# A Hyena and neighbourhood-attention step: the even half of each forward transform moved ahead by half a round, the second quarter's gates moved into the attention stage, row-wise products and outer taps on VectorE

## The chip, the cores and the metric

The kernel runs on 1 core of one Trainium2 chip. The metric is the device time of one execution in microseconds (us), lower is better. The engines are named as the profile names them: PE (TensorE, matrix products), PEld (its weight loads), DVE (VectorE), ACT (ScalarE), POOL (GpSimd) and SP (SyncE, which issues most of the transfers).

## The reference, cut to what matters

One layer of a backbone on 128 context tokens and 512 latent tokens with 1024 channels. Both token groups go through two branches that share one input projection; the kernel handles them together as rows of 640 columns (128 + 512).

```python
z = h @ w_in                              # hy, g_h, qkv, g_a, m
hy = short_conv(hy, conv_w, conv_b)       # 3 taps along the sequence
v_h, x1, x0 = split(hy, 3)
u = v_h * x1
uf = rfft(u, n=2 * L); ff = rfft(filt_full, n=2 * L)
y = irfft(uf * ff)[:, :L]                 # long convolution
y_h = (y + u * d_bias) * x0
y_a = attention(q, k, v)                  # windows and cached context keys
p_h = (y_h * silu(g_h)) @ w_bh
p_a = (y_a * silu(g_a)) @ w_ba
out = (sigmoid(m_h) * p_h + sigmoid(m_a) * p_a) @ w_out
x = layer_norm(ALPHA * x + gate * out)
```

## The kernel before, in words

All products are done in three passes of fp32r halves: a weight tile is split into a high part `wh` and a low part `wl`, the input into `hH` and `hL`, and the passes are wh·hH, wh·hL, wl·hH. A projection tile (`proj`, L184) is 128 channels by 640 tokens: 8 k-steps of 6 matmuls of 128x320, 48 in all, into two PSUM banks named `mm<i>_0` and `mm<i>_1` (pool of four banks, so two tiles at a time). Its weights come in on SP, ACT makes `wl` (a negated copy, L158), a DMA issued by POOL adds the raw tile to it (L159), and ACT makes `wh` (L160). There are two `wh` buffers, so the copy for a tile waits until the tile before the last no longer reads its own.

**The Hyena stage** goes in four rounds, a quarter q = 2 channel tiles each. `weave` (L75) lays a main chain of projections and a side chain of transforms beside each other by counting steps. The main chain of round q is `quarter_head(q + 1)` (tiles n and 8 + n, whose product is u) and `quarter_tail(q)` (L595: tiles 16 + n, which give x0, and, except where q is in `LATE_GATES`, tiles 24 + n, the gates). A `conv_tile` (L545) copies its banks to a padded row `zs` on ACT, applies the centre tap on ACT (L557) and the outer two taps either as two DVE operations (L563) or, with `taps=True`, as an ACT copy into `tap` (L560) and a POOL add (L561). `gate_tile` (L570) takes tanh on ACT (L573) and a product on DVE (L568). `gapped_product` (L538) multiplies gate row and x0 row in three POOL operations.

The side chain of round q is `gated_conv(q - 1)` (L700: transposes `yp`, `y` of the result of the last inverse transform, and products on DVE), `long_conv(q)` (L613: transposes `ut` of the rows u, split into `uh` on ACT and `ul` on DVE; class products `c0`, `s0`, then `c1`, `s1`, then `p_X`; sums and the spectrum products on DVE), and `long_conv_back(q)` braided with `filter_spectrum(q + 1)` (`fl`, `sd`, `sh`/`sl`, `fa` ... `fp`). Side products go into a second pool of four banks (`aux`, L103). In this stage the order on each engine is not written out: a scheduler with its own costs decides it from the program and its dependencies, and each engine then runs its queue strictly in that order.

**The attention stage** has 8 blocks j. In each, `attend(j)` is woven with two or three `pair_tile`s (L1183), which compute two projection tiles by a Strassen-like scheme: 7 products of 12 matmuls of 128x320 instead of 96, so 84, at the price of weight sums (L1158) and result sums (L1207, L1213) on DVE. PE's order is written out here, that of ACT and DVE is the scheduler's. `mains` (L1355) is the table of pairs by block. For the quarter in `LATE_GATES` (quarter 0 before) the x0 row is kept, the product y·x0 goes to `yu_d` in memory, and `gates_h(m)` (L1239) loads it back, multiplies by the gate and stores it to `yh_d`. `GATED_AT` (L1286) names the pairs that also compute one row of the final gate (L1307).

Of the kernel before, what the change touches and what calls it, by code (L numbers as in the profile page):

```python
# [16 lines left out]
LP = 128  # L17
# [16 lines left out]

LATE_GATES = (0,)

# [12 lines left out]
def tile_hyena_natten_step(ctx: ExitStack, tc: tile.TileContext, a, o):  # L49
# [370 lines left out]
    def filter_spectrum(q):  # L420
# [36 lines left out]
        def halves(name, sd):  # L457
            sh = hw.tile([P, 2, 256], F32R, tag="shl", bufs=4, name=f"sh{q}_{name}")
            sl = hw.tile([P, 2, 256], F32R, tag="shl", bufs=4, name=f"sl{q}_{name}")
            split(sh[:], sl[:], sd[:])  # L460
            return [(sh[:, i], sl[:, i]) for i in range(2)]
# [114 lines left out]
    def quarter_head(q):  # L576
        us = []
        out[f"u{q}"] = us
        for i in range(2):
            n = 2 * q + i  # L580
            u = hw.tile([P, ROW], F32, tag="u", bufs=4, name=f"u{n}")
            x1 = hwa.tile([P, ROW], F32, tag="cv", bufs=2, name=f"x1_{n}")
            tiles = ((n, u), (8 + n, x1))
            if q == 3 and i == 0:
                tiles = tiles[::-1]
            yield from conv_tile(*tiles[0])
            yield
            yield from conv_tile(*tiles[1])
            nc.vector.tensor_tensor(u[:, :NG], u[:, :NG], x1[:, :NG], op=ALU.mult)
            us.append(u)  # L590
            yield
# [21 lines left out]
    def long_conv(q):  # L613
        us, F, ident = out[f"u{q}"], out[f"F{q}"], out["ident"]
        if q == 0:
            dft_inverse()

# [9 lines left out]

        X = hw.tile([P, 10, 256], F32, tag="X", name=f"X{q}")
        E = out[f"E{q}"] = hw.tile([P, 12, 256], F32, tag="E", name=f"E{q}")
        e, plus, minus = E[:, :4], E[:, 4:8], E[:, 8:]  # L630
        for g in range(2):
            srcs = [src(2 * g), src(2 * g + 1)]
            yield
# [4 lines left out]
            if g == 0:  # L638
                nc.scalar.activation(e[:, 0:2], two(pc[:]), AF.Copy)
                nc.scalar.activation(e[:, 2:4], two(psn[:]), AF.Copy)  # L640
            else:
                nc.vector.tensor_tensor(plus[:, 0:2], e[:, 0:2], two(pc[:]), op=ALU.add)
                nc.vector.tensor_tensor(minus[:, 0:4:3], e[:, 0:2], two(pc[:]), op=ALU.subtract)
                nc.vector.tensor_tensor(plus[:, 2:4], e[:, 2:4], two(psn[:]), op=ALU.add)
                nc.vector.tensor_tensor(minus[:, 1:3], e[:, 2:4], two(psn[:]), op=ALU.subtract)
            yield
        s4 = src(4)
        pp = aux(f"p_X{q}")
# [19 lines left out]
    def long_conv_back(q):  # L668
# [15 lines left out]
        for g, rs_ in enumerate(((0, 2), (1, 3), (4,))):  # L684
            pb = aux(f"yb{q}_{g}")
            dst = ye[:, 2 * g : 2 * g + 2] if g < 2 else yp
            for i, r in enumerate(rs_):
                s = pq[:, r : r + 6 : 5] if r < 4 else R[:, 4:10:5]
                ph = hw.tile([P, 2, 256], F32R, tag="shl", bufs=4, name=f"ph{q}_{r}")
                pl = hw.tile([P, 2, 256], F32R, tag="shl", bufs=4, name=f"pl{q}_{r}")  # L690
# [9 lines left out]
    def gated_conv(q):  # L700
# [7 lines left out]
        for i in range(2):  # L708
# [6 lines left out]
            if q in LATE_GATES:  # L715
                x0, s0 = out["yh"][n], SC if q == 3 else GAP
                yh = hw.tile([P, ROW], F32, tag="u", bufs=4, name=f"yu{n}")[:, :NT] if q == 3 else row(yhp, "yh", f"yu{n}")
# [549 lines left out]
    def qk_(j):  # L1267
        return T_Q + j, T_K + j
# [7 lines left out]
    def mix_(m):  # L1276
# [78 lines left out]
    def mains(j):  # L1355
# [11 lines left out]
    with tc.manual_schedule(engines={mybir.EngineType.PE}):  # L1367
# [376 lines left out]
```

## Time and profile before

| | |
|---|---|
| median of 3 runs | 861.82 us (859.06, 861.82, 863.29) |
| the profiled execution, its own time | 859.01 us |
| its span in the trace | 857.0 us |
| granted clock of TensorE | 0.998 of full speed |
| PE busy / PEld busy | 847.1 / 820.6 us |
| DVE / ACT / POOL busy | 684.8 / 476.8 / 176.5 us |

The span is the time from the first to the last instruction in the trace; 2.0 us of the execution's own time lie around it. An engine's busy time counts its instructions; since consecutive instructions of ACT and DVE overlap by about a tenth of a microsecond, what one costs in a queue is read from the start of one to the start of the next in the timeline. The same holds for matmuls, whose ends are modelled.

### The profile page before, as it was taken

Reading aid. Unit: us, or ns where it says so; the run is one execution under the profiler, and the core shown is the slowest. Engines: PE = TensorE matmul, PEld = TensorE weight load, DVE = VectorE, ACT = ScalarE, POOL = GpSimd, SP = SyncE. Lnnn points to the kernel's source line nnn. Section 1 sums busy time; section 2 is a strip of 40 time slices with the busy share of each in tenths; the row PEclk is TensorE's granted clock in tenths of the full one; section 3 lists DMA queues with packets and bytes.
Section 4 is the critical chain, followed back from the end, with each engine's and each line's share of the span. In section 5 each row is a group of like instructions: output and inputs, shape, how many; then the busy total and the mean of one; then the engine's idle time right before and its main releaser. Section 6 shows DMA issues by size and latency. Waiting matters only on the chain.

```text
span 857.0 us, 16856 instructions
## 1 busy us (share of the span) xinstructions
PE 847.1 (99%) x6375; PEld 820.6 (96%) x6375; DVE 684.8 (80%) x1388; ACT 476.8 (56%) x1016; POOL 176.5 (21%) x172
## 2 busy tenths in 40 slices
PE   9999999999999999999999999999999999999996
PEld 7999999999999999999999999999999999999885
DVE  6677695597778558989988897888888668799676
ACT  4675666646557445565565576656656554345310
POOL 0010230341345201042123235124222200000000
PEclk9999999999999999999999999999999999999999
DMA  9986565666647668764353535444253375545631
GB/s 351 366 246 149 112 147 114 158 129 142 144 98 158 124 170 216 214 202 132 101 179 89 192 103 182 122 166 158 91 180 112 124 248 210 183 121 148 227 123 50
DMA packets 57443, 138.90 MB, mean 162 GB/s; under 512 B 8559, under 2 KB 24435, under 8 KB 57364
## 3 DMA queue, kind: packets, MB, share of 16 engines
q1 hardware_dynamic: 45700, 112.34, 39.6%
q0 software_dynamic: 5472, 19.14, 13.6%
q10 hardware_dynamic: 6192, 6.36, 2.1%
q8 instruction: 50, 0.82, 0.4%
q14 instruction: 29, 0.24, 0.1%
HBM read 121.04 MB, written 16.78 MB: 161 GB/s over the span
## 4 chain that ended last, share of the span: by engine, by line
PE 97%; DVE 1%; DMA 1%; SPq 0%; issue 0%; DVEq 0%
PE sp L1198 34%; PE mm L179 31%; PE out L1567 6%; PE v L934 5%; PE pt L1036 3%; PE s L1043 3%; PE s L996 2%; PE mm L193 2%; PE ve L946 1%; DMA ada<-wada 1%; PE adaT L264 1%; PE yb L169 1%; PE yb L167 1%; PE yb L168 1%; PE fl L445 1%; PE ut L622 1%
## 5 line engine op out<-in xcount | busy, mean ns | idle before, releaser
L1198 PE MATMUL sp<-t,wb 128*128 128x320 f32 x960 | 149.7, 310 | 0.0
L1198 PEld LDWEIGHTS sp<-t,wb 128*128 128x128 f32 x960 | 142.0, 188 | 1.3 <-ACT pp L1064 0.3
L1198 PE MATMUL sp<-hH,wb 128*128 128x320 f32 x480 | 116.4, 313 | 0.0
L179 PE MATMUL mm<-hH,wl 128*128 128x320 f32 x416 | 97.7, 309 | 0.0
L179 PE MATMUL mm<-hH,wh 128*128 128x320 f32 x416 | 96.9, 310 | 0.0
L179 PE MATMUL mm<-hL,wh 128*128 128x320 f32 x416 | 96.4, 309 | 0.0
L110 ACT ACTIVATE wb<-s 128x512 fp32r<-128x512 f32 x96 | 58.7, 627 | 49.3 <-DVE s L1158 25.3
L1198 PEld LDWEIGHTS sp<-hH,wb 128*128 128x128 f32 x480 | 82.4, 188 | 2.1 <-issue 2.0
L159 POOL DMA_DIRECT2D wl<-wall x35 | 30.6, 875 | 240.1 <-ACT wl L158 208.1
L1198 PE MATMUL sp<-hL,wb 128*128 128x320 f32 x240 | 74.0, 309 | 0.0
L179 PEld LDWEIGHTS mm<-hH,wl 128*128 128x128 f32 x416 | 70.3, 188 | 0.8
L179 PEld LDWEIGHTS mm<-hL,wh 128*128 128x128 f32 x416 | 69.7, 188 | 0.4
L179 PEld LDWEIGHTS mm<-hH,wh 128*128 128x128 f32 x416 | 69.6, 188 | 0.3
L111 DVE TENSOR_TENSOR wb<-s,wb 128x512 fp32r<-128x512 f32 x96 | 64.7, 686 | 6.3 <-ACT wb L110 6.2
L110 ACT ACTIVATE wb<-raw 128x512 fp32r<-128x512 f32 x69 | 43.3, 627 | 47.2 <-PE sp L1198 26.8
L160 ACT ACTIVATE wh<-raw 128x1024 fp32r<-128x1024 f32 x35 | 37.1, 1061 | 56.4 <-PE mm L179 48.2
L1018 POOL TENSOR_SCALAR p<-p,sm 128x384 f32<-128x384 f32 x32 | 44.8, 1410 | 106.1 <-DVE sm L1017 106.1
L111 DVE TENSOR_TENSOR wb<-raw,wb 128x512 fp32r<-128x512 f32 x69 | 48.3, 700 | 4.9 <-ACT wb L110 4.6
L179 PE MATMUL mm<-yhs,wh 128*128 128x320 f32 x256 | 47.9, 309 | 0.0
L1198 PEld LDWEIGHTS sp<-hL,wb 128*128 128x128 f32 x240 | 45.1, 188 | 0.0
L1213 DVE TENSOR_TENSOR c<-sp,u 128x320 f32<-128x320 f32 x72 | 34.7, 481 | 12.6 <-PE sp L1198 12.6
L1018 POOL TENSOR_SCALAR edge<-edge,sm 128x320 f32<-128x320 f32 x32 | 42.1, 1325 | 0.4 <-PE sp L1198 0.2
(397 smaller groups left out, 2133.7 us busy)
## 6 DMA issues: line engine op xcount, KB each, us to landing
raw<-wall SPq DMA_DIRECT2D x93, 512.0 KB, 3.7
wl<-wall POOLq DMA_DIRECT2D x35, 512.0 KB, 6.0
ada<-wada SPq DMA_DIRECT2D x16, 512.0 KB, 9.1
tm<-bias SPq DMA_DIRECT2D x16, 512.0 KB, 4.5
xw<-xw SPq DMA_DIRECT2D x8, 512.0 KB, 9.5
gate<-wgate SPq DMA_DIRECT2D x8, 512.0 KB, 3.8
wo<-wall SPq DMA_DIRECT2D x8, 512.0 KB, 4.5
dec<-decay SPq DMA_DIRECT2D x20, 128.0 KB, 2.2
```

Source lines behind the costliest of these rows:

```text
L110: hi = nc.scalar.activation(dst_h, src, AF.Copy)
L111: return hi, (eng or nc.vector).tensor_tensor(dst_l, src, f(dst_h), op=ALU.subtract)
L159: nc.gpsimd.dma_start(wl, a["wall"][i], accum_op=ALU.add)
L160: nc.scalar.activation(wh, raw[:], AF.Copy)
L179: nc.tensor.matmul(ps[hf][:, :HALF], wt[k], x[:, hf * HALF : (hf + 1) * HALF], start=(i == 0 and k == 0), stop=(i == lead[2] and k == NK - ...
L934: nc.tensor.matmul(ps[t // 2][:, t % 2 * 256 : t % 2 * 256 + 256], x[:, k, P * t : P * t + P], wk, start=first and t % 2 == 0, stop=last, ...
L1018: nc.gpsimd.tensor_scalar_mul(pv, pv, sm[:, 2:3])
L1036: nc.tensor.transpose(pt[:, i * P : i * P + P], x, ident)
L1043: nc.tensor.matmul(dst, lhs, rhs, start=start, stop=stop, skip_group_check=True)
L1198: nc.tensor.matmul(dst, wk, x(xi, k), start=j < 4 and k == 0 and i == 0, stop=k == 3 and i == 2, skip_group_check=True,)
L1213: after = nc.vector.tensor_tensor(c, dst, c if j == 3 else u, op=ALU.add)
L1567: ins = nc.tensor.matmul(dst, m[k][:, c0 : c0 + P], w[:, c : c + n], start=(first and k == 0), stop=(last and k == 5), skip_group_check=True,)
```

## The change

- `LATE_GATES` becomes (0, 1). The gates of quarter 1 (tiles 26 and 27, 2 x 48 matmuls) leave round 1 and come back as one `pair_tile`, `gates_h(1)` (84 matmuls), in block j = 3 of attention, which so has three pairs. The x0 rows of quarters 0 and 1 are now rows of `yhp` in the compact form (two pieces per tap, 128 and 512 columns).
- `taps=False` everywhere: the outer taps of all x0 tiles are DVE operations; the ACT copies `tap` and the POOL adds go.
- `gapped_product` (now for quarters 2 and 3 only, 4 tiles instead of 6) moves from POOL to DVE.
- `long_conv` is cut in two: `long_conv_front(q + 1)` (transposes of classes 0 to 3, products `c0`, `s0`, ACT copies into a tile `e` of its own) stands at the end of the side chain of round q; the rest stays at the head of round q + 1, behind `gated_conv(q)`. The halves `sh`, `sl`, `ph`, `pl` get six buffers instead of four.
- `EARLY_VALUES` is empty: `early_values` yields nothing.

In sum PE has 6009 matmuls instead of 6021, DVE 56 operations more, ACT 4 fewer, POOL 36 fewer (no tensor operation is left on it in the Hyena stage).

```diff
-LATE_GATES = (0,)
+LATE_GATES = (0, 1)
+EARLY_VALUES = {}
...
     def gapped_product(y, x):
-        nc.gpsimd.tensor_tensor(y[:, :LP], y[:, :LP], x[:, :LP], op=ALU.mult)
+        nc.vector.tensor_tensor(y[:, :LP], y[:, :LP], x[:, :LP], op=ALU.mult)
...
-            nc.gpsimd.tensor_tensor(ys, ys, src, op=ALU.mult)
+            nc.vector.tensor_tensor(ys, ys, src, op=ALU.mult)
...
             if q in LATE_GATES:
-                x0 = row(yhp, "yh", f"x0_{n}") if q == 3 else hwa.tile([P, ROW], F32, tag="x0", bufs=2, name=f"x0_{n}")
-                yield from conv_tile(16 + n, x0, q == 3, True)
+                x0 = row(yhp, "yh", f"x0_{n}")
+                yield from conv_tile(16 + n, x0, True, False)
...
-                yield from conv_tile(16 + n, x0, taps=True)
+                yield from conv_tile(16 + n, x0, taps=False)
...
+    def long_conv_front(q):
...
+        while len(us) < 2:
             yield
+        srcs = [src(0), src(1)]
+        yield
+        pc, psn = pairs(0, srcs)
+        e = hw.tile([P, 4, 256], F32, tag="e", name=f"e{q}")
+        nc.scalar.activation(e[:, 0:2], two(pc[:]), AF.Copy)
+        nc.scalar.activation(e[:, 2:4], two(psn[:]), AF.Copy)
+        yield
+        fronts[q] = e, [src(2), src(3)], src, pairs
+        yield
+
+    def long_conv(q):
...
+        if q not in fronts:
+            yield from long_conv_front(q)
+        e, srcs, src, pairs = fronts.pop(q)
...
+    for q in range(3):
+        weave(chain(quarter_head(q + 1), quarter_tail(q), early_values(q)), chain(gated_conv(q - 1) if q else (), long_conv(q), braid(long_conv_back(q), filter_spectrum(q + 1)), long_conv_front(q + 1)),
...
-            qk_(1), ga_(0), qk_(2), mix_(0), gh_(0), qk_(3), mix_(1), ga_(2), qk_(4), mix_(2), qk_(5), mix_(3), ga_(4), ...
+            qk_(1), ga_(0), qk_(2), mix_(0), gh_(0), qk_(3), mix_(1), ga_(2), qk_(4), mix_(2), gh_(1), qk_(5), mix_(3), ga_(4), ...
...
-            3: ((queries_keys(4), mix(2)), 2 * N_PAIR),
+            3: ((queries_keys(4), mix(2), gates_h(1)), 3 * N_PAIR),
```

The orders are read where round 1 ends and round 2 begins. Tiles 20 and 21 are the x0 tiles of quarter 2, 28 and 29 its gates (rows `yh4`, `yh5`), 22 and 30 the same of the next channel tile; `ut2_4` is the transpose of the context columns of u of quarter 2, `uh2_4` its high half.

**Place A: ACT at the gates of tile 29.** Before:

```order
L110 ACTIVATE uh2_4_2602<-ut2_4_2599 128x256
L560 ACTIVATE tap2_21_0_3141<-zs0_107,pack2_602 128x641
L160 ACTIVATE wh30_3355<-raw30_3353 128x1024
L573 ACTIVATE yh5_3162<-mm29_0_3170 128x320
L573 ACTIVATE yh5_3162<-mm29_1_3171 128x320
L158 ACTIVATE wl23_3469<-raw23_3466 128x1024
L650 ACTIVATE X2_2471<-p_X2_2606 128x2x256
```

With the change:

```order
L161 ACTIVATE wh30_3263<-raw30_3261 128x1024
L159 ACTIVATE wl23_3350<-raw23_3347 128x1024
L574 ACT_TABLE_LOAD
L574 ACTIVATE yh4_2829<-mm28_0_2837 128x320
L574 ACTIVATE yh4_2829<-mm28_1_2838 128x320
L574 ACTIVATE yh5_3056<-mm29_0_3064 128x320
L574 ACTIVATE yh5_3056<-mm29_1_3065 128x320
L111 ACTIVATE uh2_4_2421<-ut2_4_2418 128x256
L551 ACTIVATE zs1_111<-mm22_0_3160 128x128
```

The four tanh of tiles 28 and 29 stand together, behind both weight copies and behind the load of the tanh table (which before stands at tile 26, in round 1), and `uh2_4` stands behind them; before, it stood ahead of `wh30` and of the tanh of tile 29.

**Place B: PE at the same time**, from `ut2_4` to `p_X2`, which reads `uh2_4`. Before:

```order
L169 MATMUL s1_X2_2570<-uh2_3_2553,dftL_104 128x256
L622 MATMUL ut2_4_2599<-pack2_602,u4_1568 128x128
L622 MATMUL ut2_4_2599<-pack2_602,u5_1807 128x128
L179 MATMUL mm29_0_3170<-hL_89,wh29_3165 128x320
L179 MATMUL mm29_1_3171<-hL_89,wh29_3165 128x320
```

With the change:

```order
L170 MATMUL s1_X2_2389<-uh2_3_2288,dftL_104 128x256
L623 MATMUL ut2_4_2418<-pack2_602,u4_1612 128x128
L623 MATMUL ut2_4_2418<-pack2_602,u5_1840 128x128
L168 MATMUL p_X2_2425<-uh2_4_2421,dftH_103 128x256
L445 MATMUL fl3_0_2572<-w3h_3_2565,hid_94 128x512
L446 MATMUL fl3_0_2572<-w3l_3_2566,hid_94 128x512
L180 MATMUL mm22_0_3160<-hH_88,wh22_3155 128x320
```

Before, 26 projection matmuls of tile 29 stand between the transposes `ut2_4` and `p_X2`; now `p_X2` follows the transposes at once, and ahead of them stand, after the last matmul of tile 29, the ten transposes `yp1`, `y2`, `y3` and the twelve products `c1`, `s1` of quarter 2 in one piece.

**Place C: ACT at the last piece of the filter spectrum of quarter 2**, `sh2_4`, which PE's `fp2` reads. Before:

```order
L110 ACTIVATE w3h_3_2746<-w3s3_2748 128x512
L110 ACTIVATE sh2_4_2321<-sd4_2_2318 128x512
L560 ACTIVATE tap2_20_0_2908<-zs2_115,pack2_602 128x641
L160 ACTIVATE wh29_3165<-raw29_3163 128x1024
L573 ACTIVATE yh4_2911<-mm28_0_2919 128x320
```

With the change:

```order
L111 ACTIVATE w3h_3_2565<-w3s3_2567 128x512
L161 ACTIVATE wh22_3155<-raw22_3153 128x1024
L111 ACTIVATE sh2_4_2158<-sd4_2_2155 128x512
L551 ACTIVATE zs0_107<-mm21_0_2950 128x128
L553 ACTIVATE zs0_107<-mm21_0_2950 128x8x8
```

Before, `sh2_4` followed `w3h_3` at once; now the weight copy `wh22` stands between them. `wh22` takes the buffer of tile 21's weights, so it waits for that tile's matmuls.

## Rows read from the trace of the kernel before

**Rows 1.** The page: span, busy time of the engines, the chain that ended last by engine.

```profile
span 857.0 us, 16856 instructions
PE 847.1 (99%) x6375; PEld 820.6 (96%) x6375; DVE 684.8 (80%) x1388; ACT 476.8 (56%) x1016; POOL 176.5 (21%) x172
...
PE 97%; DVE 1%; DMA 1%; SPq 0%; issue 0%; DVEq 0%
```

**Rows 2.** Busy time by stretch of 40 us through the Hyena stage; last line: sums.

```profile
200.00:240.00 40.00, 40.00 (x289) 39.82 (x288) 24.21 (x46) 25.01 (x47) 8.58 (x9) 1.00 0.57 132
...
sum 320.00, PE 320.00 PEld 318.10 DVE 240.20 ACT 191.98 POOL 77.05; mean PE 40.00 PEld 39.76 DVE 30.02 ACT 24.00 POOL 9.63
```

**Rows 3.** The chain of waits: start, us, what; a projection piece and a pair piece.

```profile
686.84 28.16 PE mm L179 x192
745.01 45.78 PE sp L1198 x312
```

**Rows 4.** Timeline of PE at the end of round 1: start, us, what.

```profile
221.33 0.40 PE L445 MATMUL fl<-w3l,hid 128*128 128x512 f32 x1
221.56 0.31 PE L179 MATMUL mm<-hH,wh 128*128 128x320 f32 x1
...
222.00 0.28 PE L168 MATMUL fd<-sl,gsH 128*128 128x256 f32 x1
222.12 0.28 PE L169 MATMUL fd<-sh,gsL 128*128 128x256 f32 x1
...
228.12 0.38 PE L707 MATMUL yp<-pack,E 128*128 128x128 f32 x2
...
228.69 0.54 PE L179 MATMUL mm<-hH,wh 128*128 128x320 f32 x2
```

**Rows 5.** Timeline of DVE at the same place.

```profile
221.76 0.69 DVE L450 TENSOR_TENSOR sd<-fl,dec 128x512 f32<-128x512 f32 x1 [1.51 <-PE fl L445]
222.37 0.75 DVE L436 TENSOR_TENSOR w3s<-w 128x256 f32<-128x256 f32 x2
```

**Rows 6.** Timeline of ACT at the same place.

```profile
223.57 0.67 ACT L110 ACTIVATE w3h<-w3s 128x512 fp32r<-128x512 f32 x1
224.09 0.67 ACT L110 ACTIVATE sh<-sd 128x512 fp32r<-128x512 f32 x1
```

**Rows 7.** Timeline of ACT where tile 26's gates load the tanh table.

```profile
155.56 1.07 ACT L160 ACTIVATE wh<-raw 128x1024 fp32r<-128x1024 f32 x1 [1.37 <-PE mm L179]
156.53 1.04 ACT L158 ACTIVATE wl<-raw 128x1024 fp32r<-128x1024 f32 x1
157.59 1.28 ACT L573 ACT_TABLE_LOAD   x1
158.88 0.77 ACT L573 ACTIVATE yh<-mm 128x320 f32<-128x320 f32 x2
159.53 0.60 ACT L519 ACTIVATE F<-fp 128x512 f32<-128x512 f32 x1
```

**Rows 8.** Groups of ACT, 40 to 360 us: busy, mean ns, idle before.

```profile
L160 ACT ACTIVATE wh<-raw 128x1024 fp32r<-128x1024 f32 x35 | 37.1, 1061 | 56.4 <-PE mm L179 48.2 <-PE ve L946 7.4 <-PE mm L193 0.7
L110 ACT ACTIVATE uh<-ut 128x256 fp32r<-128x256 f32 x20 | 7.3, 395 | 9.6 <-PE ut L622 9.4
```

**Rows 9.** Groups of DVE in the same stretch.

```profile
L111 DVE TENSOR_TENSOR sl<-sd,sh 128x512 fp32r<-128x512 f32 x24 | 24.0, 1000 | 13.5 <-ACT sh L110 13.4
L563 DVE SCALAR_TENSOR_TENSOR x<-zs,pack,x 128x641 f32<-128x641 f32 x16 | 14.1, 882 | 1.9 <-ACT x L557 1.7
```

**Rows 10.** Groups of POOL in the same stretch.

```profile
L561 POOL TENSOR_TENSOR x<-x,tap 128x641 f32<-128x641 f32 x16 | 30.2, 1887 | 11.5 <-ACT tap L560 11.5
L543 POOL TENSOR_TENSOR yh<-yh,x 128x448 f32<-128x448 f32 x6 | 8.7, 1449 | 0.2 <-DVE yh L568 0.2
```

**Rows 11.** Busy time in attention: block 1 (three pairs) and block 3 (two).

```profile
401.00:447.00 46.00, 45.95 (x362) 44.52 (x358) 40.39 (x101) 27.61 (x71) 11.62 (x10) 1.00 0.43 139
...
493.00:528.00 35.00, 35.00 (x287) 33.82 (x286) 31.39 (x89) 24.25 (x64) 12.10 (x10) 1.00 0.51 155
```

**Rows 12.** Groups of DVE, 400 to 800 us.

```profile
L111 DVE TENSOR_TENSOR wb<-s,wb 128x512 fp32r<-128x512 f32 x86 | 57.9, 686 | 5.2 <-ACT wb L110 5.1
...
L1213 DVE TENSOR_TENSOR c<-sp,u 128x320 f32<-128x320 f32 x65 | 31.3, 482 | 12.6 <-PE sp L1198 12.6
```

**Rows 13.** The chain of waits inside block 1: a run of pieces on DVE.

```profile
413.77 0.49 DVE c L1213
...
418.60 0.69 DVE wb L111
```

More of the change, by code (lines that the diff above doesn't have):

```diff
@@ L457, in halves @@
         def halves(name, sd):
-            sh = hw.tile([P, 2, 256], F32R, tag="shl", bufs=4, name=f"sh{q}_{name}")
-            sl = hw.tile([P, 2, 256], F32R, tag="shl", bufs=4, name=f"sl{q}_{name}")
+            sh = hw.tile([P, 2, 256], F32R, tag="shl", bufs=6, name=f"sh{q}_{name}")
+            sl = hw.tile([P, 2, 256], F32R, tag="shl", bufs=6, name=f"sl{q}_{name}")
             split(sh[:], sl[:], sd[:])
@@ L576, in quarter_head @@
     def quarter_head(q):
-        us = []
-        out[f"u{q}"] = us
+        us = out.setdefault(f"u{q}", [])
         for i in range(2):
@@ L611, in quarter_tail @@
             yield
[L613 to L616, printed above, removed]
+    fronts = {}
+    def long_conv_front(q):
+        ident = out["ident"]
+        us = out.setdefault(f"u{q}", [])
         def src(cls):
@@ L626, in src, with pairs @@
             return (uh[:], ul[:]), (uh[:], ul[:])
[L628 to L633, printed above, removed]
+        def pairs(g, srcs):
             pc = aux(f"c{g}_X{q}")
@@ L637, in long_conv @@
                 dft_pair((pc[:, 256 * i : 256 * i + 256], psn[:, 256 * i : 256 * i + 256]), 2 * g + i, *srcs[i])
[L638 to L645, printed above, removed]
-            yield
+            return pc, psn
+        while len(us) < 2:
+            yield
+        srcs = [src(0), src(1)]
[8 more added lines that the diff above has]
+    def long_conv(q):
+        F = out[f"F{q}"]
+        if q == 0:
+            dft_inverse()
+        if q not in fronts:
+            yield from long_conv_front(q)
+        e, srcs, src, pairs = fronts.pop(q)
+        X = hw.tile([P, 10, 256], F32, tag="X", name=f"X{q}")
+        E = out[f"E{q}"] = hw.tile([P, 12, 256], F32, tag="E", name=f"E{q}")
+        plus, minus = E[:, 4:8], E[:, 8:]
+        pc, psn = pairs(1, srcs)
+        nc.vector.tensor_tensor(plus[:, 0:2], e[:, 0:2], two(pc[:]), op=ALU.add)
+        nc.vector.tensor_tensor(minus[:, 0:4:3], e[:, 0:2], two(pc[:]), op=ALU.subtract)
+        nc.vector.tensor_tensor(plus[:, 2:4], e[:, 2:4], two(psn[:]), op=ALU.add)
+        nc.vector.tensor_tensor(minus[:, 1:3], e[:, 2:4], two(psn[:]), op=ALU.subtract)
+        yield
         s4 = src(4)
@@ L688, in long_conv_back @@
                 s = pq[:, r : r + 6 : 5] if r < 4 else R[:, 4:10:5]
-                ph = hw.tile([P, 2, 256], F32R, tag="shl", bufs=4, name=f"ph{q}_{r}")
-                pl = hw.tile([P, 2, 256], F32R, tag="shl", bufs=4, name=f"pl{q}_{r}")
+                ph = hw.tile([P, 2, 256], F32R, tag="shl", bufs=6, name=f"ph{q}_{r}")
+                pl = hw.tile([P, 2, 256], F32R, tag="shl", bufs=6, name=f"pl{q}_{r}")
                 split(ph[:], pl[:], s)
@@ L715, in gated_conv @@
             if q in LATE_GATES:
-                x0, s0 = out["yh"][n], SC if q == 3 else GAP
+                x0, s0 = out["yh"][n], SC
                 yh = hw.tile([P, ROW], F32, tag="u", bufs=4, name=f"yu{n}")[:, :NT] if q == 3 else row(yhp, "yh", f"yu{n}")
@@ L918, in values @@
         if m:
-            v = [slot(0, t, f"v{m}{t}")[:, :n] for t, n in (("k", 512), ("kl", 768))]
-            v = [v[0], v[1][:, :512], v[1][:, 512:]]
+            if m in EARLY_VALUES.values():
+                v = hwa.tile([P, 1280], F32, tag="dinv", name=f"vs{m}")
+                v = [v[:, 512 * i : min(512 * i + 512, 1280)] for i in range(3)]
+            else:
+                v = [slot(0, t, f"v{m}{t}")[:, :n] for t, n in (("k", 512), ("kl", 768))]
+                v = [v[0], v[1][:, :512], v[1][:, 512:]]
         else:
@@ L958, in tile_hyena_natten_step, with early_values @@
     N_VALUES = 11
+    def early_values(q):
+        if q in EARLY_VALUES:
+            yield from values(EARLY_VALUES[q])
+    for q in range(3):
+        weave(chain(quarter_head(q + 1), quarter_tail(q), early_values(q)), chain(gated_conv(q - 1) if q else (), long_conv(q), braid(long_conv_back(q), filter_spectrum(q + 1)), long_conv_front(q + 1)),
+              (6 if q in LATE_GATES else 8) * NK + N_VALUES * (q in EARLY_VALUES), N_GATED * min(q, 1) + N_CONV + N_BACK + N_FILTER)
     def hand_over():
@@ L1285, in tile_hyena_natten_step @@
     follow = {x: y for run in runs for x, y in zip(run, run[1:])}
-    GATED_AT = [runs[0][i][0] for i in (0, 1, 2, 3, 6, 7, 8, 9, 11, 12, 13, 14, 16, 17, 18, 19)]
+    GATED_AT = [runs[0][i][0] for i in (0, 1, 2, 3, 6, 7, 8, 9, 12, 13, 14, 15, 17, 18, 19, 20)]
     weave(hand_over(), chain(gated_conv(2), long_conv(3), long_conv_back(3), gated_conv(3), attention_setup(), late_sums()),
@@ L1375, in tile_hyena_natten_step @@
                 values_back(j // 2 + 1)
-            weave(chain(*main), attend(j), n_main, N_ATT if j < 7 else N_ATT + 3, 1 if j in (1, 2, 4, 6) else 0)
+            weave(chain(*main), attend(j), n_main, N_ATT if j < 7 else N_ATT + 3, 1 if j in (1, 2, 3, 4, 6) else 0)
     ac.close()
```

5 lines of the change are left out of this document (1 added, 4 removed).

## The prediction

> **What bounds the kernel now.** The page comes first [rows 1]: PE is busy for 847.1 of 857.0 us, and 97% of the chain that ended last is PE. The reader is to see that a change can gain only matmuls that it removes, and can lose only where it makes PE wait. The table of busy time by stretch says where PE waits now [rows 2]: through the whole Hyena stage nowhere (320.00 of 320.00 us), while DVE is busy for 240, ACT for 192 and POOL for 77 of those 320. PE is never granted less than full clock in the rows of the stretches [rows 2, 11]. So work that goes from POOL to DVE costs nothing in the mean. What matters is the order: PE runs its queue strictly, and one late operand is a hole that nothing fills. The timelines show what each step in such an order takes, from start to start [rows 4 to 7].
>
> **The matmuls.** The two tiles of quarter 1's gates take 2 x 48 matmuls of 128x320 as direct projections and 84 as a pair. A projection matmul takes 28.16 / 192 = 0.1467 us on the chain, a pair matmul 45.78 / 312 = 0.1467 [rows 3]. The gain is 12 x 0.1467 = **1.76 us**. All other PE work is the same in number; moving the front of the transform changes only its place.
>
> **Taps and gate-row products.** DVE takes over the outer taps of the eight x0 tiles that ACT and POOL shared, 16 operations of 0.88 us [rows 9], in compact pieces for quarter 1, about 14 us, and about 4 us of products (4 tiles, each one of 128, 64 and 448 columns; the nearest DVE price is by columns, 0.48 us for 320 [rows 12], so about 1 us for each tile). It gets back time that it now loses beside POOL: the 24 splits `sl` take 1.00 us in the mean where the same size takes 0.69 in attention [rows 9, 12], 7 us, and POOL's 30.2 and 8.7 us of tensor operations are gone [rows 10]. Net some 10 us more on DVE over 320 us in which it is idle for 80 [rows 2]. Cost: 0. The cover is DVE's idle time; the place where it could be thin is the start of a quarter's inverse transform, but there the sums now come earlier, since the even half of the forward transform is already done. On ACT, 16 copies `tap` go. ACT's wait for POOL's adds ahead of them goes too.
>
> **Transfers.** `gates_h(1)` adds two loads on SP and four half-row stores on ACT's queue, and two weight tiles leave POOL's queue of DMA-adds. The loads wait for rows that were stored some 200 us earlier; the DMA engines are busy for about half the time there [rows 11]. Cost 0, from 0 to 0.3.
>
> **Place C, `sh2_4` behind `wh22`.** Let T be the start of the last matmul of `fl2_4`. Before PE gets to `fp2` it issues that one (0.23), 16 projection matmuls (2.35) and nine transform matmuls (1.08, at 0.12 each): T + 3.66 [rows 4]. DVE starts `sd` at T + 0.43 and ends the sums `w3s` at T + 1.79 [rows 4, 5]; ACT's `w3h` is done at T + 2.46 [rows 6]. `wh22` waits for the last use of tile 21's high weights, 13 matmuls behind the `fl`: T + 0.23 + 13 x 0.147 + 0.31 = T + 2.45. So `wh22` starts at about T + 2.46, `sh2_4` 0.97 later [rows 7], and 0.67 after that it is there [rows 6]: T + 4.10. PE waits 0.4 us. Bounds: 0 (a scheduler that meant this order may know that `fl` is late anyway) to 1.0 (if the copies of tile 21's banks, queued behind, add 0.5). I take **0.4**.
>
> **Places A and B, `uh2_4` behind four tanh.** Let S be the start of the last two matmuls of tile 29. PE then has those two (0.29), ten transposes (six take 0.57 [rows 4], so 0.95), twelve products (1.43) and two transposes (0.19): it stands before `p_X2` at S + 2.86. ACT starts `wh30` when the last use of the tile's high weights ends, S + 0.16; `wl23` follows 0.97 later, the table load 1.06 later, the first tanh 1.29 later; a tanh takes 0.325, so four 1.30 [rows 7]; `uh2_4` takes 0.40 [rows 8]. It is there at S + 5.18. PE waits **2.3 us**, since `p_X2` is at the head and nothing behind it may pass, not even tile 22, whose bank is free by then. Bounds: 0, if ACT gets to `wh30` or the load earlier than its queue says, which nothing in the rows supports; 3.5, if the two weight copies and DVE's gate products behind the tanh come in full behind each other. In the trace of before the same load stands in front of tile 26's tanh, with projections for PE to do meanwhile, and PE had no hole there [rows 2, 7].
> The Trainium skill has a rule that makes this dearer: ScalarE: Activation LUTs, section "What ACT_TABLE_LOAD costs", gives about 1.28 us for the load and about 1.38 us more for a drain, at every switch to another set. The trace agrees on the load (1.28 [rows 7]) and shows no such drain: the copy ahead ends at 157.57, the load starts at 157.59, and tanh follows 0.01 us behind it. By the rule the wait would be 3.7 and the sum 1.4 us higher; by the rows it is 2.3, and the measurement decides.
>
> **Block 3 of attention with three pairs.** The nearest row is block 1, which has the same three kinds of pair: PE 45.95 of 46.00 us, DVE 40.39 [rows 11]. I take its loss, **0.05**. Below: 0. Above: block 1's chain runs over DVE from 413.77 to 419.29 [rows 13], so PE has no slack there, and a pair needs 11 x 0.69 + 13 x 0.48 = 13.8 us of DVE [rows 12] beside 12.35 of PE: 31.39 + 13.8 = 45.2 in a block of 47.35. If those 5.5 us became idle PE, the loss would be 5.5.
>
> **The sum** on the profiled execution, 859.01 us (a span of 857.0 and 2.0 around it): -1.76 + 0 + 0.4 + 2.3 + 0.05 = +1.0, so 860.0. That execution lay 2.81 below the median of the runs shown, 861.82; carried over, **862.8**. A measurement of this kernel can tell about 0.5% (4.3 us) from no change, so the forecast is within it: what the pair saves is lost again at two places where ACT is late.
>
> **Rivals.**
> 1. No holes: ACT is in time, or the holes are filled. For it: PE has no hole in 320 us before [rows 2], and the scheduler that set that order set this one too. Against: the walk above uses only measured steps, and ACT's own queue gives no earlier start. It gives -1.76: 857.3, or **860.1** at the median.
> 2. Slower: DVE sets the pace of block 3. Place: the sums and weight splits of `gates_h(1)`, which follow those of `mix(2)` without a light pair between. Price: up to 5.5 us [rows 13], with the holes: -1.76 + 2.7 + 5.5 = +6.4, **868.3**. It decides once DVE is busy for more than about 95% of the block; the sum above has 45.2 of 47.35. Against: block 1 has the same load and loses 0.05.
> 3. The change does not do what it says: the front is "half a round early" only in the program; in PE's queue of the change `c0`, `s0` stand only a few us earlier against the projections than before. I take this as true in part: it is why I count no gain for it. Were it to matter, it would be at the end of the stage, where the last inverse transform now ends about 6 us of PE work further ahead of the first pair; no wait stands there now, so it gives 0.
> 4. Both holes at their upper bounds and a third of the same kind at another quarter: -1.76 + 1.0 + 3.5 + 2.5 = +5.2, **867.1**.
>
> **How the numbers follow.** My forecast has 0.60, rival 1 0.20 (with 3 in it), rival 2 0.10, rival 4 0.10. The runs shown spread by 2.8 below and 1.5 above their median, so each case carries about 2 us either way. The range for 8 in 10 runs from 858.2 (rival 1 less 1.9) to 866.5 (the forecast with place A and C at their bounds, +1.8, and 1.9 more), and leaves out most of rivals 2 and 4. Faster by over 0.5% would be under 857.5: only rival 1 with a low run, 0.04. Slower means over 866.1: most of rivals 2 and 4, 0.14. The rest, 0.82, is within 0.5%.
>
> **What would show it.** Right: in the timeline of PE two holes at the end of round 1 and the start of round 2, about 0.4 us in front of `fp` and 2 to 2.5 us in front of `p_X`, released by ACT's `sh` and `uh`; ACT_TABLE_LOAD once, there, with four tanh behind it; PE in the 40 us around it at 37 to 38; 12 matmuls fewer; `sl` back at 0.69 us; no POOL tensor operation. Wrong: PE at 40.00 in every stretch (rival 1), a wait of PE on DVE's splits in block 3 (rival 2), or a third hole at a quarter's turn (rival 4).

## The result, and the profile after

The changed kernel takes 863.6 us in the median (22 executions, 861.5 to 867.28), before took 859.93 (22 executions, 859.0 to 863.29). The ratio is 1.0037, with a 95% interval of 1.0027 to 1.0048: 3.2 us slower by the ratio, 3.7 between the medians, in either case within the 0.5% that the forecast counts as no change, and inside its range (858.2 to 866.5, with 862.8 as the likeliest).

The page of the profiled execution (864.05 us), span, busy time and chain, beside [rows 1]:

```profile
span 862.1 us, 16843 instructions
PE 850.3 (99%) x6363; PEld 821.6 (95%) x6363; DVE 696.4 (81%) x1444; ACT 466.0 (54%) x1008; POOL 132.2 (15%) x136
...
PE 95%; DVE 3%; ACT 1%; issue 1%; DVEq 0%; ACTq 0%
```

PE is busy for 3.2 us more although it has 12 matmuls fewer, and PE's share of the chain falls from 97 to 95%: DVE has 3% of it, ACT 1%. The table by stretch (start, PE, PEld, DVE, ACT, POOL, granted clock) shows where, beside [rows 2]:

```profile
200.00:240.00 40.00, 37.60 (x270) 36.79 (x269) 26.10 (x53) 23.27 (x43) 3.46 (x4) 1.00 0.55 123
240.00:280.00 40.00, 40.00 (x287) 39.65 (x286) 35.60 (x60) 19.09 (x34) 3.49 (x4) 1.00 0.61 136
...
360.00:400.00 40.00, 39.82 (x304) 38.02 (x303) 37.81 (x104) 26.24 (x76) 17.22 (x15) 1.00 0.53 160
```

Between 200 and 240 us PE is busy for 37.60 of 40.00; before, no stretch there was under 40.00. Between 360 and 400, where attention begins, a little is missing too. What PE waited for in the whole execution (us in total, times, longest):

```profile
PE p_X L168 <- ACT uh L111: 2.1, 1, 2.1
PE mm L284 <- DVE hid L276: 1.2, 1, 1.2
PE fp L168 <- ACT sh L111: 0.3, 1, 0.3
PE sp L1224 <- DVE wb L112: 0.2, 1, 0.2
```

The second line is in the prologue, and before had it too; the other three are new. The two in the Hyena stage, in PE's timeline:

```profile
223.62 0.28 PE L170 MATMUL fd<-sh,gsL 128*128 128x256 f32 x1
224.21 0.39 PE L168 MATMUL fp<-sh,dftH 128*128 128x256 f32 x1 [0.31 <-ACT sh L111]
...
237.07 0.28 PE L170 MATMUL s_X<-uh,dftL 128*128 128x256 f32 x1
237.19 0.38 PE L623 MATMUL ut<-pack,u 128*128 128x128 f32 x2
239.66 0.39 PE L168 MATMUL p_X<-uh,dftH 128*128 128x256 f32 x1 [2.09 <-ACT uh L111]
239.88 0.39 PE L445 MATMUL fl<-w3h,hid 128*128 128x512 f32 x1
```

and in ACT's:

```profile
222.59 1.05 ACT L161 ACTIVATE wh<-raw 128x1024 fp32r<-128x1024 f32 x1
223.54 0.61 ACT L111 ACTIVATE sh<-sd 128x512 fp32r<-128x512 f32 x1
...
234.58 1.06 ACT L161 ACTIVATE wh<-raw 128x1024 fp32r<-128x1024 f32 x1 [0.26 <-PE mm L180]
235.54 1.05 ACT L159 ACTIVATE wl<-raw 128x1024 fp32r<-128x1024 f32 x1
236.61 1.28 ACT L574 ACT_TABLE_LOAD   x1
237.90 1.43 ACT L574 ACTIVATE yh<-mm 128x320 f32<-128x320 f32 x4
239.19 0.41 ACT L111 ACTIVATE uh<-ut 128x256 fp32r<-128x256 f32 x1
```

PE issues the last product ahead of `fp` at 223.62 and `fp` itself at 224.21, 0.47 later than the 0.12 that a product takes; ACT's `wh` copy (222.59) stands ahead of `sh` (223.54), as place C said. At places A and B PE has issued the two transposes `ut` by 237.38 and starts `p_X` at 239.66, 2.28 later. ACT goes through `wh`, `wl`, the table load, four tanh and `uh` from 234.58 to 239.60 without a gap, from start to start 0.96, 1.07, 1.29, 1.29 as read before [rows 7].

**Two starts.** The profiled execution of the change also began more slowly. PE's timeline of before, then of after:

```profile
4.03 0.87 PE L230 MATMUL ps_f<-zemb,pack 33*64 33x320 f32 x4
...
9.29 0.81 PE L230 MATMUL ps_f<-hf,pack 64*128 64x320 f32 x4
```

```profile
4.04 1.33 PE L231 MATMUL ps_f<-zemb,pack 33*64 33x320 f32 x4
...
11.42 1.44 PE L231 MATMUL ps_f<-hf,pack 64*128 64x320 f32 x4
```

The same four filter products take 0.87 and 1.33 us, the next four 0.81 and 1.44; after 15 us both run alike, but the one is 2.76 us behind: the first `fl` product is issued at 48.09 us in before, at 50.85 in after, which also lengthens PE's busy time. The instructions are the same. The executions of before fall into two groups, 859.00 to 859.94 (12 of 22) and 861.49 to 863.29 (10), with nothing between; of the twelve profiled executions of this case, seven issue their first `fl` product at 48.1 to 49.1 us, five at 50.6 to 51.5. So the change is better read from the first `fl` product to the end of the span. For after:

```profile
50.85 0.39 PE L445 MATMUL fl<-w3h,hid 128*128 128x512 f32 x1
...
359.34 0.31 PE L1224 MATMUL sp<-hH,wb 128*128 128x320 f32 x1
```

It took 857.04 - 48.09 = 808.95 us in before and 862.12 - 50.85 = 811.27 in after, **+2.3 us**. The first pair product (`sp`, 359.34 in after, 367.61 in before) splits that. Hyena: 308.49 us, plus the 96 matmuls that left (14.08), makes 322.57 beside 319.52, so +3.05. Attention and the rest: 502.78, less 84 matmuls (12.32), makes 490.46 beside 489.43, so +1.03. The 12 matmuls are -1.76.

### The profile page after: what moved, and what is told of

Its sections match the earlier page's. It is cut to its first block, busy times and chain, and to the rows that moved or that the text cites. A ratio compares the mean times of both kernels' runs of the same rounds, so it can differ in the third digit from the quotient of the medians.

```text
span 862.1 us, 16843 instructions
## 1 busy us (share of the span) xinstructions
PE 850.3 (99%) x6363; PEld 821.6 (95%) x6363; DVE 696.4 (81%) x1444; ACT 466.0 (54%) x1008; POOL 132.2 (15%) x136
## 4 chain that ended last, share of the span: by engine, by line
PE 95%; DVE 3%; ACT 1%; issue 1%; DVEq 0%; ACTq 0%
PE sp L1224 33%; PE mm L180 29%; PE out L1593 6%; PE v L952 5%; PE s L1069 3%; PE pt L1062 2%; PE s L1022 2%; PE mm L194 2%; PE ve L964 1%; PE adaT L265 1%; DVE wb L112 1%; PE mm L284 1%; PE yb L169 1%; PE yb L168 1%; PE ut L623 1%; DVE s L1184 1%
## 5 line engine op out<-in xcount | busy, mean ns | idle before, releaser
L1224 PE MATMUL sp<-t,wb 128*128 128x320 f32 x1008 | 158.0, 310 | 0.3 <-DVE wb L112 0.2
L1224 PEld LDWEIGHTS sp<-t,wb 128*128 128x128 f32 x1008 | 149.1, 188 | 2.4 <-DVE wb L112 1.1
L1224 PE MATMUL sp<-hH,wb 128*128 128x320 f32 x504 | 121.6, 312 | 0.0
L180 PE MATMUL mm<-hH,wh 128*128 128x320 f32 x384 | 92.0, 309 | 0.0
L180 PE MATMUL mm<-hL,wh 128*128 128x320 f32 x384 | 91.6, 310 | 0.0
L180 PE MATMUL mm<-hH,wl 128*128 128x320 f32 x384 | 90.5, 309 | 0.0
L1224 PEld LDWEIGHTS sp<-hH,wb 128*128 128x128 f32 x504 | 86.5, 188 | 2.0 <-issue 2.0
L180 PEld LDWEIGHTS mm<-hH,wh 128*128 128x128 f32 x384 | 65.3, 188 | 0.3
L180 PEld LDWEIGHTS mm<-hL,wh 128*128 128x128 f32 x384 | 65.1, 188 | 0.4
L180 PEld LDWEIGHTS mm<-hH,wl 128*128 128x128 f32 x384 | 65.0, 188 | 0.5
```

The source lines that it names most:

```text
L180: nc.tensor.matmul(ps[hf][:, :HALF], wt[k], x[:, hf * HALF : (hf + 1) * HALF], start=(i == 0 and k == 0), stop=(i == lead[2] and k == NK - ...
L1224: nc.tensor.matmul(dst, wk, x(xi, k), start=j < 4 and k == 0 and i == 0, stop=k == 3 and i == 2, skip_group_check=True,)
```

## The experiments

All ran on chips beside before, and all are read in that way. The change has three parts that can be put in one by one: **G**, the second quarter of late gates; **F**, the early front; **D**, taps and products on DVE (the rest on ACT and POOL). "Hyena" and "attention" are the differences to before as just worked out; G gains 1.76 beside them.

| kernel | parts | median, ratio to before (95%) | first `fl` to end | Hyena | attention |
|---|---|---|---|---|---|
| before | none | | 808.95 | 0 | 0 |
| d_only | D | 865.93, 1.0060 (1.0040 to 1.0081) | 814.11 | +4.84 | +0.31 |
| f_only | F | 861.96, 1.0022 (1.0008 to 1.0036) | 810.72 | +1.51 | +0.26 |
| g_only | G | 869.32, 1.0101 (1.0081 to 1.0121) | 818.07 | +10.05 | +0.83 |
| undo_f | G, D | 862.58, 1.0029 (1.0018 to 1.0040) | 811.55 | +0.63 | +3.73 |
| undo_d | G, F | 859.85, 0.9991 (0.9977 to 1.0005) | 807.65 | -0.09 | +0.55 |
| undo_g | F, D | 860.56, 1.0000 (0.9987 to 1.0014) | 809.36 | +0.43 | -0.02 |
| after | G, F, D | 863.6, 1.0037 (1.0027 to 1.0048) | 811.27 | +3.05 | +1.03 |
| x_table | all, load early | 860.48, 1.0011 (0.9996 to 1.0026) | 810.24 | +1.64 | +1.41 |
| x_all | all, both holes closed | 861.63, 1.0004 (0.9992 to 1.0016) | 808.86 | +0.61 | +1.06 |
| x_gbc | x_all, gate row moved | 861.24, 0.9998 (0.9982 to 1.0013) | 808.35 | +0.70 | +0.46 |
| best2 | undo_d, gate row moved | 859.98, 0.9984 (0.9967 to 1.0000) | 808.37 | -0.09 | +1.26 |

Medians go by which of the two starts an execution had; the fourth column does not. But one trace stands behind each figure of the last three columns. As a check: in the nine changed kernels whose execution times split into two groups, the medians of the lower group give the differences to before of the fourth column again to within 0.7 us (after +2.5 for +2.3, x_gbc -1.25 for -0.60), so a smaller difference between two rows counts only where the traces show its place.

The rows differ in one more thing. The halves `sh`, `sl`, `ph`, `pl` have four buffers in before, d_only and g_only, five in f_only, undo_d and best2, and six in the others. No run separates the buffers from the parts, so a difference between two such rows can hold a share of theirs.

**x_table: the table load alone.**

```diff
                 yield from conv_tile(16 + n, x0, True, False)
+                if n == 0:
+                    early_tanh = hwa.tile([P, 1], F32, tag="et", name="early_tanh")
+                    nc.scalar.activation(early_tanh[:], x0[:, 0:1], AF.Tanh)
```

> The changed kernel with one ACT instruction more: a tanh of one column, early in the stage, whose result nobody reads, so that the tanh table is loaded near 100 us instead of in front of the gates of quarter 2. The order at the two holes is otherwise the same. My theory (PE waits for ACT's queue, and the load of 1.28 us is part of what stands in front of uh2_4): PE's wait before p_X falls from 2.1 us to 0.8, the wait before fp stays at 0.3, and the kernel is 1.3 us faster than the changed one, about 862.3 beside 863.6. Rival (VectorE's added work is what costs; ACT's lateness is covered or comes back later): the wait before p_X shrinks but the end does not move, 863.6. Rival (the difference is the slower start that the profiled run of the change had, 2.8 us before 50 us): no difference in the median either, only in the mix of starts.

PE's waits in its profile:

```profile
PE p_X L168 <- ACT uh L111: 0.7, 1, 0.7
PE fp L168 <- ACT sh L111: 0.3, 1, 0.3
PE sp L1227 <- DVE wb L112: 0.2, 1, 0.2
```

The wait before `p_X` is 0.7 us, that before `fp` is as it was. From the first `fl` the kernel is 1.0 us faster than the change: the Hyena stage gained 1.4, about the load's 1.28, and attention lost 0.4 more this time. The load is on the path, and the rival that nothing moves at the end is out; so is the start as the whole difference, since this reading begins behind it.

**x_all: both holes.** With the edit of x_table; the lines that set `marks` are left out here.

```diff
...
+            copy = nc.scalar.activation(wh, raw[:], AF.Copy)
+            if i in (22, 30):
+                behind(copy, marks["sh2_4" if i == 22 else "uh2_4"])
+            if i == 30:
+                behind(copy, marks["yh5"])
...
```

> As the kernel with the early tanh, and in addition two orders on ACT set by hand: the weight copy of tile 22 behind sh2_4, the weight copy of tile 30 behind the tanh of tile 29 and uh2_4. My theory: the wait before fp is gone (0.3 to 0), the wait before p_X is under 0.5, PE is busy for 40.00 of 40 us between 200 and 240 us or nearly so, and the kernel is 2.2 to 2.7 us faster than the changed one: about 861.1, still not faster than before by what can be told, since 1.0 us more was lost in attention. Rival (VectorE): no more than 0.5 us faster than the changed kernel. A new hole where the copy of tile 30 is late would show as a wait of PE at its first matmul and would take back up to 1 us.

```profile
200.00:240.00 40.00, 40.00 (x289) 39.57 (x287) 28.52 (x57) 23.06 (x44) 3.45 (x4) 1.00 0.54 120
```

PE is busy for 40.00 of 40.00 us, neither `fp` nor `p_X` waits, and from the first `fl` it is 2.4 us faster than the change, as expected: the two holes were 2.75 us by the timeline. What is left against before is Hyena +0.6 and attention +1.06, which eat the 1.76.

**undo_f: without the early front.** 
```diff
-    ... braid(long_conv_back(q), filter_spectrum(q + 1)), long_conv_front(q + 1)),
+    ... braid(long_conv_back(q), filter_spectrum(q + 1))),
```

> The change without the early front: the even half of each forward transform is back at the head of its own round; the gates of quarter 1 in attention and the work on VectorE stay. In ACT's order uh2_4 now stands behind the weight copies of tiles 30, 23 and the four tanh too, but on PE other work can lie between ut2_4 and p_X. My theory: what matters is whether PE has work at that place, so no hole over 0.5 us there, and the kernel is 2 us faster than the changed one, about 861.5. Rival (VectorE's load costs): no difference to the changed kernel, since all the added work is still there. Rival (the early front is a gain that other losses hide): slower than the changed kernel.

Half right. The holes are gone (Hyena +0.63), but from the first `fl` the kernel is 0.3 us slower than the change, not 2 us faster: attention lost 3.73 us. PE's timeline at its start:

```profile
368.71 1.00 PE L1224 MATMUL sp<-t,wb 128*128 128x320 f32 x5 [0.89 <-DVE t L112]
...
375.41 0.56 PE L1224 MATMUL sp<-t,wb 128*128 128x320 f32 x2 [0.87 <-ACT wb L111]
```

The first pairs wait for DVE's `t`, the late sums, and for ACT's `wb`. So the front does give something: it brings the last inverse transform, and with it the sums that attention needs, forward. The last transposes `y` stand 18.0 us ahead of the first pair product in after, 11.2 us in undo_f; the last late sum `t` starts 4.3 and 13.0 us behind it.

**undo_g: without the second quarter of late gates.** 
```diff
-LATE_GATES = (0, 1)
+LATE_GATES = (0,)
...
-            3: ((queries_keys(4), mix(2), gates_h(1)), 3 * N_PAIR),
+            3: ((queries_keys(4), mix(2)), 2 * N_PAIR),
```

> The change without the second quarter of late gates: tiles 26 and 27 are direct projections in round 1 again, block 3 of attention has two pairs; early front and VectorE's work stay. The tanh table is loaded at tile 26 again. My theory: the 1.76 us of matmuls come back, the hole before p_X is gone since the load and two of the four tanh no longer stand in front of uh2_4 (-2.1), block 3's loss of about 0.4 is gone: 0.5 to 1 us faster than the changed kernel. Rival (VectorE's load costs): about 2 us slower than the changed kernel, since the gates of quarter 1 bring six gapped products more on VectorE into the stage and the matmuls come back.

It is 1.9 us better than the change, more than expected; no wait of PE is left but that of the prologue, and attention is at before's time. VectorE's rival, slower than the change, is out.

**d_only, f_only, g_only, undo_d: the rest of the eight combinations.** d_only is before with the `+` lines here, f_only and undo_d have the `-` lines in the changed kernel (f_only also the edit of undo_g); g_only is undo_d without the call of the front. The quarters in `LATE_GATES` have the same switch of `taps`, left out here, and the numbers of buffers are those named above.

```diff
-        nc.gpsimd.tensor_tensor(y[:, :LP], y[:, :LP], x[:, :LP], op=ALU.mult)
+        nc.vector.tensor_tensor(y[:, :LP], y[:, :LP], x[:, :LP], op=ALU.mult)
...
-                yield from conv_tile(16 + n, x0, taps=True)
+                yield from conv_tile(16 + n, x0, taps=False)
```

> Before, with only the work moved to VectorE: outer taps of all x0 tiles and the gate-row products. Read from the first fl matmul to the end (so that a slow or a quick start of the prologue drops out), before took 808.95 us. My theory: VectorE has idle time for it through the stage, +0 to +0.3, but the run without the early front lost 2.7 us at the start of attention to VectorE's late sums, so with the same load and no early front I now expect a part of that here: +0.5 to +2, as waits of the first pair products on VectorE's t and wb. Rival (VectorE's load never matters by itself; it was the shorter lead in front of attention that the two missing tiles leave): 0.

> Before, with only the early front (and x0 of quarter 0 in the compact form, five buffers for the halves instead of six for lack of space). My theory: the front gives nothing by itself where nothing waits, 0 to +0.4 us from the first fl to the end (808.95 before); no hole before p_X, since the tanh table is loaded at tile 26. Rival (the front is the harmful part): +1 us or more with holes where ACT is late. Rival (the front is the gain): under 808.5.

> Before, with only the second quarter of late gates. 12 matmuls fewer: -1.76. Theory: on ACT the four tanh and the table load stand together again in front of other work, but on PE 24 projection matmuls lie between ut2_4 and p_X, so the hole is small: -1.5 to +0.5 us against before (808.95 from the first fl to the end). Rival (late gates cost more in attention than they save, since block 3 gets VectorE's 13.8 us): +1 us or more, with waits in blocks 0 to 3.

> The change with its work on VectorE undone: taps as ACT copies and POOL adds, products on POOL (five buffers for the halves instead of six, for space). On ACT the table load and the tanh of tile 28 stand in front of uh2_4, the weight copy of tile 30 behind it; on PE 24 projection matmuls stand between ut2_4 and p_X. Theory: no hole over 0.3 us in the Hyena stage, and the wait at 382 us (block 0 of attention, 0.55 us) gone since VectorE comes in earlier: 807.5 to 808.5 from the first fl to the end, the best of the eight combinations, 0.5 to 1.4 us better than before. Rival (the work on VectorE is the part that helps): slower than the changed kernel's 811.27.

d_only lost 5.2 us, far more than any theory said, and not at the start of attention (+0.31) but in the Hyena stage, at the turn to its last round. By start-to-start times about 4.5 of the 4.84 us lie between 306 and 318. From 306.60 to 312.95 PE's queue holds only steps of the transforms; before has value products `v` between such steps, here these stand behind:

```profile
308.38 0.66 PE L714 MATMUL y<-pack,E 128*128 128x128 f32 x4 [0.25 <-ACT F L519]
...
310.27 0.36 PE L167 MATMUL c_X<-uh,dftH 128*128 128x256 f32 x1 [0.31 <-DVE yh L729]
311.39 0.35 PE L167 MATMUL s_X<-uh,dftH 128*128 128x256 f32 x1 [0.77 <-DVE yh L729]
311.97 0.38 PE L168 MATMUL c_X<-ul,dftH 128*128 128x256 f32 x1 [0.22 <-DVE ul L111]
```

PE waits there for ACT's copy `F`, for DVE's products `yh` and for its halves `ul`, one behind the other. And it pays twice, since the clock falls behind the hole (start, PE, PEld, DVE, ACT, POOL, granted clock):

```profile
308.00:310.00 2.00, 1.54 (x10) 1.02 (x8) 2.00 (x8) 0.71 (x2) 0.00 (x0) 1.00 0.00 0
310.00:312.00 2.00, 0.74 (x3) 0.40 (x3) 2.00 (x8) 0.72 (x2) 0.00 (x0) 1.00 0.41 164
312.00:314.00 2.00, 2.00 (x14) 2.00 (x15) 0.60 (x2) 1.42 (x4) 0.00 (x0) 0.79 0.78 291
314.00:316.00 2.00, 2.00 (x11) 2.00 (x11) 0.08 (x1) 1.34 (x3) 0.00 (x0) 0.50 0.58 216
316.00:318.00 2.00, 2.00 (x17) 2.00 (x17) 0.42 (x1) 0.62 (x2) 0.00 (x0) 0.86 0.17 58
```

At 0.79, 0.50 and 0.86 for 2 us each PE loses by estimate 0.85 x 2 = 1.7 us more. g_only has that hole too, at 300 us, with the same waits (0.25, 0.31 and 0.77 us), although its taps and products are on ACT and POOL: the hole goes with the order, and VectorE's added work is not needed for it. g_only has others where ACT is late, the longest of them:

```profile
PE ut L623 <- ACT F L520: 2.3, 1, 2.3
PE fp L168 <- ACT sh L111: 0.9, 1, 0.9
```

So the expectation for g_only (-1.5 to +0.5) failed by far: +9.1, in the Hyena stage and not in blocks 0 to 3. That for f_only (0 to +0.4) failed too: it lost 1.8 us, of which the waits view names only 0.4 (`ve` on DVE's `kl`), and no late ACT, as its rival had it; the rest was not traced further. undo_d is the only one of the eight combinations under before: 807.65, 1.3 us less, as expected. No hole in the Hyena stage, and none in block 0:

```profile
200.00:240.00 40.00, 40.00 (x292) 39.74 (x291) 25.33 (x53) 26.02 (x47) 13.07 (x14) 1.00 0.53 127
...
360.00:400.00 40.00, 40.00 (x305) 38.98 (x304) 37.01 (x99) 25.29 (x72) 16.20 (x14) 1.00 0.38 114
```

So no part has a price of its own. D costs 5.2 us alone, 3.6 on top of G and F, and takes 6.5 off G; F costs 1.8 alone and gains 10.4 beside G. Each part makes the scheduler draw another order, and where the traces were walked the price is what holes that order has.

**x_gbc: VectorE in block 0.** From x_all.

```diff
-    GATED_AT = [... (0, 1, 2, 3, 6, 7, 8, 9, 12, 13, 14, 15, 17, 18, 19, 20)]
+    GATED_AT = [... (1, 2, 3, 6, 7, 8, 9, 12, 13, 14, 15, 16, 17, 18, 19, 20)]
```

> The kernel with both holes closed (early tanh, orders on ACT by hand), and the first row of the final gate taken out of block 0 of attention (block 6 gets three rows, block 0 one). Theory: the 0.55 us that PE loses in block 0 are VectorE at its limit there, and 1.0 us of work less ends the wait: attention costs +0.5 instead of +1.06 over before's rows (from the first pair matmul to the end, the 84 added matmuls taken off), and 808.3 from the first fl to the end instead of 808.86. Rival (the order in that block, not the load): no change, 808.9. The added row in block 6 can cost up to 0.3.

The wait at the start of attention is gone, attention costs +0.46 and the kernel takes 808.35, both as expected. So the 1.07 us of that row on DVE stood in front of what PE waited for, and the rival that nothing changes is out. But taking the row out also made the scheduler draw another order on DVE behind it, and DVE is as busy as before in the 23 us up to that place (22.36 us, as in x_all); load and order are not separated here.

**best2: VectorE in block 3.** From undo_d.

```diff
-    GATED_AT = [... (0, 1, 2, 3, 6, 7, 8, 9, 12, 13, 14, 15, 17, 18, 19, 20)]
+    GATED_AT = [... (0, 1, 2, 3, 6, 7, 8, 11, 12, 13, 14, 15, 17, 18, 19, 20)]
```

> The change with taps and products back on ACT and POOL, and one row of the final gate moved from block 3, which now has three pairs, to block 4's first pair. Theory: block 3 loses 0.40 us because a third pair beside two gate rows is more than VectorE can do there; with one row less (1.3 us of VectorE) the loss is under 0.15, so 807.3 to 807.5 from the first fl to the end instead of 807.65, and 1.5 us better than before, the best version so far: about 0.998 of before. Rival (the loss in block 3 comes from the order of the pair's weight sums): no change, 807.65.

Block 3 still loses as much, so the expectation failed. The trace shows what the loss is, one short wait of PE's weight load for a split on DVE, in after (below), in undo_d at 497.54 and in best2 at 500.80 alike:

```profile
503.81 1.32 PEld L1224 LDWEIGHTS sp<-t,wb 128*128 128x128 f32 x9 [0.31 <-DVE wb L112]
```

The row that best2 moves away stands behind that place (505.99 in after); the one ahead of it (493.54) stayed. So this run could not tell load from order, and that stays open. Attention was 0.7 worse than undo_d's, 0.5 of it at the very end of the kernel (792.5 us in before's time), far from the edit.

## Why the prediction was right, and where it was not

- **-1.76 for the matmuls**: as counted; nothing in the runs speaks against it. **Transfers, 0**: no wait of PE for a transfer is among those listed for the change.
- **Place C, 0.4**: the timeline has 0.47. **Places A and B, 2.3**: it has 2.28. x_table and x_all show that ACT's order is the cause, and that the time comes back. The rule on the table load that was weighed against this (Trainium skill, ScalarE: Activation LUTs, "What ACT_TABLE_LOAD costs") would have had a drain of 1.38 us more. This trace does not agree: the copy ahead ends at 236.59, the load starts at 236.61, and tanh follows it at 237.90.
- **Taps and products, 0**: wrong, and this is the step that failed: "Cost: 0. The cover is DVE's idle time". Two sizes were right: the taps in one piece cost 0.88 us each, and `sl` fell from 1.00 to 0.69 us, 7.5 us in all (7 said). The net was not: 10 us more on DVE were said for the stage, but from the first `fl` to the first pair product it is busy for 237.9 us in after, 235.9 in undo_d, which differs by D and one buffer, and 240.4 in before. Other operations got shorter too (`X` from `E`, 0.84 to 0.68 us). The 11.6 us by which DVE's busy time grows in the whole kernel lie in attention (14.0 more), with its additional pair. The two sizes:

```profile
L564 DVE SCALAR_TENSOR_TENSOR x<-zs,pack,x 128x641 f32<-128x641 f32 x24 | 21.1, 880 | 5.3 <-ACT x L558 5.1
L112 DVE TENSOR_TENSOR sl<-sd,sh 128x512 fp32r<-128x512 f32 x24 | 16.5, 686 | 13.1 <-ACT sh L111 13.1
```

  So the load came out smaller than said, and the cover failed even so: idle time in a stretch of 40 us is no cover at the place where PE turns to attention. There the chain goes over DVE (start, us, what):

```profile
376.50 1.20 DVE wb L112 x2
377.70 0.85 DVE s L1184
...
381.36 0.61 DVE wb L112
```

  PE waits until 382.01; by the next pair products it is 0.55 us behind before's, product by product. In the 23 us of attention up to there DVE is busy for 22.3 us in after, for 20.9 in undo_d, which has +0.02 there; x_gbc has none. x_all also keeps +0.61 in the Hyena stage where undo_d has -0.09; that this is D's as well is argued from the two alone, and was not traced piece by piece.
- **Block 3, 0.05**: 0.28 in after, 0.31 in undo_d and best2 over the block, by the alignment of the products (0.1 more at the worst place in it). Block 1 as the nearest row was too kind; the load came out like block 1's (below: DVE 41.48 of 47.00), so the load was not the measure. Rival 2's wait, PE for DVE's splits, is there (best2 above), at 0.3 us and not 5.5.

```profile
493.00:540.00 47.00, 46.95 (x368) 45.52 (x367) 41.48 (x104) 28.29 (x73) 14.34 (x11) 1.00 0.44 141
```

- **Rival 3, "it gives 0"**: wrong. I read the end of the stage from a trace in which nothing waited there. With the front the kernel is 10.4 us faster beside G alone (g_only to undo_d) and 4.8 beside D alone (d_only to undo_g), in both cases with more buffers too, and 0.3 beside both (undo_f to after).
- **The sum**: +1.0 predicted from the first `fl` to the end, +2.3 measured; the 1.3 missing are block 0 (0.55), block 3 (0.3) and 0.3 to 0.4 in the Hyena stage. The predicted median rested on the offset of 2.81 us between one execution and the median of three; with 22 executions before is at 859.93, 1.9 lower. So 862.8 came near 863.6 by errors that cancel: the base 1.9 too high, the sum 1.3 too small, and 1.4 that is left, which fits executions of the change that began slowly more often (17 of 22 are at 863.29 or above, three of them at 866.5 to 867.28, of which no trace is kept). That it came so near is luck. Whether that mix is the change's doing is open: by their times x_table had the slow start in 4 of 12, x_all in 7 of 12.

## What to carry to other kernels

Where one engine is at 99%, walk its queue at the places where the order changed, instruction by instruction, with start-to-start times of both queues: the two holes came out to 0.1 us. Mean idle time did not cover the turn to attention here: ask of each helper engine how far it is behind at the turn between two stages, where the bottleneck engine has no other work to put in. And an edit that a scheduler sees is priced only together with the others: the same part cost 5.2 us or took 6.5 off.

If a version is wanted: the change without its work on VectorE (undo_d) is 1.3 us better than before and 3.6 better than the change from the first `fl` to the end, though its ratio to before, 0.9991, has an interval that includes 1; best2 comes out at 0.9984 with an interval that ends at 1.0000.

## What the runs showed of the hardware

Behind d_only's hole the granted clock fell to 0.50, the lower of its two levels, 1.2 GHz (the table above); behind the change's, which is no shorter, it stayed at 1.00, 2.4 GHz:

```profile
236.00:238.00 2.00, 1.57 (x14) 1.33 (x12) 2.00 (x7) 1.97 (x3) 0.86 (x1) 1.00 0.60 88
238.00:240.00 2.00, 0.34 (x2) 0.35 (x3) 1.89 (x5) 1.60 (x5) 0.00 (x0) 1.00 0.96 367
240.00:242.00 2.00, 2.00 (x15) 1.92 (x14) 2.00 (x8) 0.00 (x0) 0.00 (x0) 1.00 1.10 253
```

In d_only PE was busy for 1.54 and 0.74 of 2 us, in pieces, and then granted 0.79, 0.50 and 0.86; in after it was busy for 1.57 and 0.34 of 2 us, in one piece, and then granted 1.00. g_only has both in one execution: from 228 to 236 us PE was idle for 3.5 of 8 us, most of it in one piece of 2.29, and the clock stayed at 1.00; from 300 to 304 it was busy for 1.57 and 0.93 of 2 us, in pieces, and was granted 0.84 from 302, then 0.50 and 0.81. What decides between them no run here tells. In the two starts the profile's granted clock reads 1.00 in both, so it does not show why the same products took longer; that stays open as well.
